# Encoder, mixer A: rotary sines through a second, pair-swapped copy, and the product with v for two heads at a time

## The chip, the core and the metric

The kernel runs on one core of a Trainium2 chip. The metric is the device time of one execution in microseconds (us). A core has five engines with a queue of instructions each, worked off in order: TensorE (PE in the profile; its weight loads are shown as PEld), VectorE (DVE), ScalarE (ACT), GpSimd (POOL) and SyncE (SP), which here only starts transfers. Matmuls write to PSUM, which ScalarE and VectorE can read; all else is in SBUF.

## The reference

A trunk of two layers over 256 positions of width 2048, in float32. Layer 0 mixes tokens with mixer A, layer 1 with mixer B; after each comes a gated MLP with a depthwise convolution. The change lies in mixer A alone: grouped-query attention with 16 query heads, 4 heads for k and v, head width 128, normalised q and k, and a rotation by position of each half of a head.

```python
def rot(xs, pos):                      # a half of a head, 64 wide; quarter = 32
    ang = pos[:, None] * inv_freq[None, :]
    x1, x2 = xs[..., :quarter], xs[..., quarter:]
    return jnp.concatenate([x1 * cos - x2 * sin, x2 * cos + x1 * sin], axis=-1)
...
q = axial_rope(rms_norm(q, q_gain)); k = axial_rope(rms_norm(k, k_gain))
logits = jnp.einsum('bqkgd,bskd->bkgqs', q_blk, k) * scale
p = jax.nn.softmax(logits, axis=-1)
o = jnp.einsum('bkgqs,bskd->bqkgd', p, v)
```

So each element of the rotated q or k is itself times a cosine plus its partner, 32 columns away, times a sine with a sign.

## The kernel before

Each float32 factor is split into a high part in a reduced format and the low rest, and a product is made of three matmuls (high by high, low by high, high by low). Weights stream from HBM in pieces of 128 x 1024 (`raw`, four buffers); ScalarE writes the high part `wh` (L156), VectorE the rest `wl` (L157), four buffers each. `feed` uses a piece in 12 matmuls (L144 to L146) that add into two accumulators in PSUM, `acc`, one for each half of the 256 positions (m = 0, 1).

Mixer A projects k and v first, then q in four groups of four heads. What follows a projection is written as a generator, and between matmuls of the next projection `step()` takes it to its next `yield`, so that the small work runs beside the next group's weights. A scheduler then orders each engine's queue by its own estimates; weight splits have a higher priority.

After k or a group of q, `qk_post` runs:

- ScalarE writes `stg`, the accumulators times the token's scale (L477, two activations of 512 columns), and `sq`, their squares (L591).
- GpSimd multiplies `stg`, with pairs swapped, by the signed sines `st` into `t2`: four operations of 256 columns (L597), one for each m and each half of a pair.
- VectorE multiplies `stg` by the cosines `ct` into `ro` (L600), adds `t2` (L602), sums the squares by head (L603) and prepares the norm (L272), which GpSimd finishes with a power (L273).

For a group of q, `attend` transposes `ro` on TensorE (L494), splits it into `qT` (L196 on ScalarE, L197 on VectorE), and then goes through six steps, k = 0 to 5, in two halves each. In the first half of step k it computes the scores of head k (L210 to L212, 6 matmuls), the maximum on VectorE (L646, L648), the exponential on ScalarE (L652), and the division by the sum on GpSimd (L656). In the second half, head k-1's probabilities are transposed on TensorE (L665) and split into `pT` (two buffers), and head k-2's product with v runs: 6 matmuls of 256 columns (L210 to L212, via `mm3`) into a PSUM tile of its own, split into the head's slots `ah`, `al`. A group's last steps fall into the projection of the next group, whose `qk_post` is queued between them.

The tables of cosines and sines are made at the start from `rp` (the rope table) and `gbs` (the gains), which share buffers with `pT`.

Of the kernel before, what the change touches and what calls it, by code (L numbers as in the profile page):

```python
# [7 lines left out]
F32 = mybir.dt.float32  # L8
F32R = mybir.dt.float32r
AF = mybir.ActivationFunctionType  # L10
ALU = mybir.AluOpType
AX = mybir.AxisListType

P = 128
D = 2048
NT = 256
# [12 lines left out]
def tile_encoder(ctx: ExitStack, tc: tile.TileContext, x, xT, w_a, w_ao, q_gain, k_gain, w_b, w_bo,  # L29
                 rel_bias, gains, w_up, conv, w_down, final_norm, rope, ident_c, onehot, out):  # L30
    nc = tc.nc
# [24 lines left out]
    def nm(s):  # L56
        uid[0] += 1
        return f"{s}_{uid[0]}"

    def ps_tile():  # L60
        return psp.tile([P, 512], F32, tag="ps", name=nm("ps"))
# [3 lines left out]
    def copy(o, i):  # L65
        turn[0] ^= 1
        if turn[0]:
            nc.scalar.activation(o, i, AF.Copy)
        else:
            nc.vector.tensor_copy(o, i)  # L70
# [121 lines left out]
    def split(hi, lo, src):  # L192
        if lo is None:
            copy(hi, src)
            return
        nc.scalar.activation(hi, src, AF.Copy)  # L196
        nc.vector.tensor_tensor(lo, src, hi.bitcast(F32), ALU.subtract)  # L197
# [7 lines left out]
    def mm3(o, lhsT, rhs, ls, rs, start, stop):  # L205
        (lh, ll), (rh, rl) = lhsT, rhs
        if ll is None:
            nc.tensor.matmul(o, lh[ls], rh[rs], start=start, stop=stop)  # L208
            return
        nc.tensor.matmul(o, lh[ls], rh[rs], start=start, stop=False)  # L210
        nc.tensor.matmul(o, lh[ls], rl[rs], start=False, stop=False)  # L211
        nc.tensor.matmul(o, ll[ls], rh[rs], start=False, stop=stop)  # L212

    def pair_tile(pool, shape, tag, bufs=1, whole=False):
        if whole:
            return pool.tile(shape, F32, tag=tag + "h", name=nm(tag), bufs=bufs), None
        return tuple(pool.tile(shape, F32R, tag=tag + c, name=nm(tag + c), bufs=bufs) for c in "hl")
# [9 lines left out]
    def new_slots(kts):  # L227
        return {kt: new_slot(kt) for kt in kts}
# [40 lines left out]
    def rsqrt_mean(dst, ss, n, eps=EPS):  # L269
        w = ss.shape[-1]  # L270
        ms = small.tile([P, w], F32, tag="ms", name=nm("ms"))
        nc.vector.tensor_scalar(ms, ss, 1.0 / n, eps, op0=ALU.mult, op1=ALU.add)  # L272
        nc.gpsimd.tensor_tensor(dst, ms, nhalf[:, :w], ALU.pow)  # L273
# [200 lines left out]
    def evac_scaled(pool, accs, rstd, bufs=2):  # L474
        o = pool.tile([P, 2, 512], F32, tag="stg", name=nm("stg"), bufs=bufs)
        for m in range(2):
            nc.scalar.activation(o[:, m, :], accs[m], AF.Copy, scale=rstd[:, m:m + 1])  # L477
        return o

    def evac_split(pool, accs, rstd, whole=False):  # L480
        hi, lo = pair_tile(pool, [P, 2, 512], "v", 1, whole)
        for m in range(2):
            split_scaled(hi[:, m, :], lo if lo is None else lo[:, m, :], accs[m], rstd[:, m:m + 1])
        return hi, lo
# [25 lines left out]
    def mixer_a():  # L510
        with tc.tile_pool(name="apool", bufs=1) as ap:
# [1 line left out]
            hT, ss_in = {}, new_ss()  # L513
            kgs = list(range(4))

            rp = ap.tile([P, 2, 2, P], F32, tag="pTh", name="rp", bufs=2)
            gbs = ap.tile([P, 4, P], F32, tag="pTl", name="gbs", bufs=2)
            tabs = {}
            rstd = []

# [59 lines left out]
                    load_x(1)  # L580

            def qk_post(accs, which, keep, scale=1.0):
                s = evac_scaled(ap, accs, rstd[0], 1)
                ct, st = tabs[which]
                ssq = small.tile([P, 8], F32, tag="ssq", name=nm("ssq"))
                r = small.tile([P, 8], F32, tag="rqk", name=nm("rqk"), bufs=3)
                ro = ap.tile([P, 2, 512], F32, tag="ro", name=nm("ro"))
                t2 = ap.tile([P, 2, 512], F32, tag="t2", name=nm("t2"))
                sq = ap.tile([P, 2, 512], F32, tag="sq", name=nm("sq"))
                for m in range(2):  # L590
                    nc.scalar.activation(sq[:, m, :], accs[m], AF.Square, scale=rstd[0][:, m:m + 1])  # L591
                rv, sv = (t.rearrange("p m (a c) -> p m a c", a=4) for t in (ro, s))
                for m in range(2):
                    t5, s5 = (t[:, m, :].rearrange("p (a f e c) -> p a f e c", a=4, f=2, e=2) for t in (t2, s))
                    st5 = st[:, m, :].rearrange("p (f e c) -> p f e c", f=2, e=2)
                    for e in range(2):
                        nc.gpsimd.tensor_tensor(t5[:, :, :, e, :], s5[:, :, :, 1 - e, :],  # L597
                                                st5[:, None, :, e, :].to_broadcast([P, 4, 2, 32]), ALU.mult)
                yield
                nc.vector.tensor_tensor(rv, sv, ct[:, :, None, :].to_broadcast([P, 2, 4, P]), ALU.mult)  # L600
                yield
                nc.vector.tensor_tensor(ro, ro, t2, ALU.add)  # L602
                nc.vector.tensor_reduce(ssq, sq.rearrange("p m (a c) -> p (m a) c", a=4), axis=AX.X, op=ALU.add)  # L603
                rsqrt_mean(r, ssq, P * scale * scale, EPS / (scale * scale))
                keep.extend((ro, r))

            slots = new_slots(range(16))
# [15 lines left out]
            v = evac_split(ap, va, rstd[0])  # L623
# [3 lines left out]
            def attend(g, accs):  # L627
                keep = []
                yield from qk_post(accs, "q", keep, SCALE)
                ro, rq = keep  # L630
                rqv = rq.rearrange("p (m a) -> p m a", m=2)
                qT = pair_tile(ap, [P, 4, NT], "qT")
                yield
                for _ in heads_T(qT, ro):
                    pass
                prs, pTs, ots = {}, {}, {}
                for k in range(6):
                    yield
                    if k < 4:
                        i = k  # L640
                        s = ps_tile()
                        for m in range(2):
                            mm3(s[:, m * NT:(m + 1) * NT], qT, kT,
                                (slice(None), i, slice(m * P, (m + 1) * P)), (slice(None), g), True, True)
                        mx = small.tile([P, 2], F32, tag="mx", name=nm("mx"), bufs=3)
                        nc.vector.tensor_reduce(mx, s.rearrange("p (m c) -> p m c", m=2), axis=AX.X,  # L646
                                                op=ALU.max, negate=True)
                        nc.vector.tensor_tensor(mx, mx, rqv[:, :, i], ALU.mult)  # L648
                        pr = ap.tile([P, 2, NT], F32, tag="pr", name=nm("pr"), bufs=2)
                        l = small.tile([P, 2], F32, tag="l", name=nm("l"), bufs=3)  # L650
                        for m in range(2):
                            nc.scalar.activation(pr[:, m, :], s[:, m * NT:(m + 1) * NT], AF.Exp,  # L652
                                                 bias=mx[:, m:m + 1], scale=rq[:, 4 * m + i:4 * m + i + 1],
                                                 accum_out=l[:, m:m + 1])
                        nc.vector.reciprocal(l, l)
                        nc.gpsimd.tensor_tensor(pr, pr, l[:, :, None].to_broadcast([P, 2, NT]), ALU.mult)  # L656
                        prs[i] = pr
                    yield "half"
                    if 1 <= k < 5:
                        i = k - 1  # L660
                        pr = prs.pop(i)
                        t = ps_tile()
                        for m in range(2):
                            for kt in range(2):
                                nc.tensor.transpose(t[:, kt * NT + m * P:kt * NT + (m + 1) * P],  # L665
                                                    pr[:, m, kt * P:(kt + 1) * P], ident)
                        pTs[i] = pair_tile(ap, [P, 2 * NT], "pT", 2)
                        split(pTs[i][0], pTs[i][1], t)
                    if k >= 2:
                        i = k - 2  # L670
                        pT = pTs.pop(i)
                        ot = ps_tile()[:, :NT]
                        for kt in range(2):
                            mm3(ot, v, pT, (slice(None), kt, slice(g * P, (g + 1) * P)),
                                (slice(None), slice(kt * NT, (kt + 1) * NT)), kt == 0, kt == 1)
                        hi, lo = slots[4 * g + i]
                        split(hi, lo, ot)

            for g in range(4):
                start(attend(g, project(w_a, g, hT, kgs)))  # L680
# [258 lines left out]
```

## Time and profile before

| | us |
|---|---|
| median of 3 runs (2294.59 to 2295.15) | 2294.7 |
| the profiled execution | 2294.99 |
| its span, first to last instruction | 2293.2 |
| TensorE busy | 2280.3 |
| VectorE busy | 1631.3 |
| ScalarE busy | 1218.1 |
| GpSimd busy | 170.3 |

How to read it: an engine's busy time is the union of its instructions' times. A matmul's time includes its way through the array and overlaps with its neighbours', so the start of one to the start of the next says what it costs in a run. In a row of groups stand line, engine, operation, output <- inputs, shape and count, then busy us and mean ns, then the idle time before them and what ended it. In a row of the timeline stand start us, duration us, engine, line, operation, and the idle time before it with its releaser. In a row of waits stand who waited for whom, us in total, times and the longest. In a row of stages stand the stretch, its length, then busy us and count for PE, PEld, DVE, ACT and POOL, TensorE's granted clock, the share of the DMA engines and GB/s. A row of one line's instructions gives the shortest, median and longest in ns, then the first and last start. In the critical chain stand start, duration and what.

### The profile page before, as it was taken

The page shows a single profiled execution, that of the slowest core. Times are in us where ns is not written, and L with a number is a line of the kernel's source. Part 1 is how long each engine was busy: PE and PEld are TensorE (multiplying, and loading weights), DVE is VectorE, ACT ScalarE, POOL GpSimd, SP SyncE. Part 2 cuts the span into 40 slices and gives each one's busy share as a digit, 9 for nine tenths or more (in the row PEclk, how much of TensorE's full clock was granted, in tenths as well). Part 3 has the DMA queues.
Part 4 walks back from the last instruction along what each step waited for, and adds up shares of the span by engine and source line. Part 5 has one row for each costly group of instructions (what it writes and reads, how often), then busy time and mean ns, then how long its engine had stood idle before and what let it go on. Part 6 is the DMA issues. An engine that isn't in the chain of part 4 may idle for free.

```text
span 2293.2 us, 31100 instructions
## 1 busy us (share of the span) xinstructions
PE 2280.3 (99%) x11641; PEld 1947.1 (85%) x11641; DVE 1631.3 (71%) x2284; ACT 1218.1 (53%) x1746; POOL 170.3 (7%) x170
## 2 busy tenths in 40 slices
PE   9999999999999999999999999999999999999998
PEld 7888888888888888888888888888888888888886
DVE  6877877776457776878866875676777744777754
ACT  7565565554345555545454554445555533555543
POOL 2331101110000000010000000000000000000010
PEclk9999999999999999999999999999999999999999
DMA  8535656765555555566555554566555565555554
GB/s 299 166 131 164 202 190 206 214 213 194 194 194 184 192 190 189 188 216 210 185 175 181 178 189 163 178 198 206 189 189 189 188 194 193 191 190 187 192 191 149
DMA packets 261447, 437.57 MB, mean 191 GB/s; under 512 B 17216, under 2 KB 198208, under 8 KB 261168
## 3 DMA queue, kind: packets, MB, share of 16 engines
q1 hardware_dynamic: 254912, 425.64, 56.6%
q0 software_dynamic: 5952, 9.38, 1.6%
q8 instruction: 91, 1.49, 0.3%
q10 hardware_dynamic: 432, 0.56, 0.1%
q14 instruction: 60, 0.49, 0.1%
HBM read 429.20 MB, written 6.29 MB: 190 GB/s over the span
## 4 chain that ended last, share of the span: by engine, by line
PE 97%; DVE 1%; DMA 0%; issue 0%; POOL 0%; ACT 0%; SPq 0%; POOLq 0%; DVEq 0%; ACTq 0%
PE acc L123 28%; PE acc L145 17%; PE acc L146 17%; PE acc L144 17%; PE acc L121 15%; PE ps L208 1%; PE ps L211 1%; PE ps L212 0%; PE ps L210 0%; DMA raw<-in_w_a_dram 0%; DVE wl L157 0%; PE ps L665 0%; PE ps L815 0%; DVE tT L237 0%; POOL t L597 0%
## 5 line engine op out<-in xcount | busy, mean ns | idle before, releaser
L157 DVE TENSOR_TENSOR wl<-raw,wh 128x1024 fp32r<-128x1024 f32 (+1 forms) x456 | 553.5, 1216 | 320.1 <-ACT wh L156 316.2
L156 ACT ACTIVATE wh<-raw 128x1024 fp32r<-128x1024 f32 (+1 forms) x456 | 475.0, 1045 | 514.5 <-PE acc L146 449.6
L123 PE MATMUL acc<-xh,wh 128*128 128x512 f32 x2816 | 674.2, 391 | 0.0
L123 PEld LDWEIGHTS acc<-xh,wh 128*128 128x128 f32 x2816 | 517.0, 188 | 99.9 <-DVE v L356 0.4
L112 DVE TENSOR_TENSOR wl<-raw,wh 128x1024 fp32r<-128x1024 f32 x352 | 457.9, 1301 | 196.6 <-ACT wh L111 196.6
L111 ACT ACTIVATE wh<-raw 128x1024 fp32r<-128x1024 f32 x352 | 372.0, 1058 | 208.4 <-issue 70.9
L144 PE MATMUL acc<-wh,ah 128*128 128x512 f32 x1024 | 399.3, 390 | 0.0
L145 PE MATMUL acc<-wl,ah 128*128 128x512 f32 x1024 | 398.8, 389 | 0.0
L146 PE MATMUL acc<-wh,al 128*128 128x512 f32 x1024 | 398.7, 389 | 0.0
L121 PEld LDWEIGHTS acc<-xh,wl 128*128 128x128 f32 x2816 | 361.8, 191 | 14.2
L121 PE MATMUL acc<-xh,wl 128*128 128x256 f32 x2816 | 366.7, 283 | 0.0
L144 PE MATMUL acc<-wh,xh 128*128 128x512 f32 x768 | 302.7, 395 | 1.9 <-ACT wh L156 1.9
L145 PE MATMUL acc<-wl,xh 128*128 128x512 f32 x768 | 300.0, 391 | 0.2 <-DVE wl L157 0.2
L146 PE MATMUL acc<-wh,xh 128*128 128x512 f32 x768 | 299.8, 390 | 0.0
L146 PEld LDWEIGHTS acc<-wh,al 128*128 128x128 f32 x1024 | 192.2, 188 | 40.0
L144 PEld LDWEIGHTS acc<-wh,ah 128*128 128x128 f32 x1024 | 192.3, 188 | 39.4
L145 PEld LDWEIGHTS acc<-wl,ah 128*128 128x128 f32 x1024 | 192.3, 188 | 39.3
L146 PEld LDWEIGHTS acc<-wh,xh 128*128 128x128 f32 x768 | 144.2, 188 | 30.4
L144 PEld LDWEIGHTS acc<-wh,xh 128*128 128x128 f32 x768 | 144.4, 188 | 30.0 <-ACT wh L156 2.3
L145 PEld LDWEIGHTS acc<-wl,xh 128*128 128x128 f32 x768 | 144.4, 188 | 27.8 <-DVE wl L157 0.5
L375 POOL TENSOR_TENSOR cv<-cg,cv 128x512 f32<-128x512 f32 x44 | 63.5, 1444 | 1101.9 <-DVE cv L367 1101.9
L355 ACT ACTIVATE v<-acc 128x256 f32<-128x256 f32 x176 | 65.8, 374 | 108.5 <-PE acc L123 108.5
(156 smaller groups left out, 1385.8 us busy)
## 6 DMA issues: line engine op xcount, KB each, us to landing
raw<-in_w_up_dram SPq DMA_DIRECT2D x352, 512.0 KB, 3.7
raw<-in_w_down_dram SPq DMA_DIRECT2D x176, 512.0 KB, 3.6
raw<-in_w_b_dram SPq DMA_DIRECT2D x144, 512.0 KB, 3.8
raw<-in_w_bo_dram SPq DMA_DIRECT2D x48, 512.0 KB, 3.6
raw<-in_w_a_dram SPq DMA_DIRECT2D x40, 512.0 KB, 4.3
raw<-in_w_ao_dram SPq DMA_DIRECT2D x32, 512.0 KB, 3.7
raw<-in_w_a_dram SPq DMA_DIRECT2D x16, 256.0 KB, 6.1
h<-in_x_dram SPq DMA_DIRECT2D x4, 512.0 KB, 7.9
```

What stands on the lines that cost most here:

```text
L111: nc.scalar.activation(wh, rk, AF.Copy)
L112: nc.vector.tensor_tensor(wl, rk, wh.bitcast(F32), ALU.subtract)
L121: nc.tensor.matmul(acc[j][:, :NT], wl[:, kt, c], lhs[4 * kg + kt][0], start=st, stop=sp)
L123: nc.tensor.matmul(acc[j], wh[:, kt, c], lhs[4 * kg + kt][2], start=st, stop=sp)
L144: nc.tensor.matmul(accs[m], xh[:, c], wh[:, j, :], start=st, stop=False)
L145: nc.tensor.matmul(accs[m], xh[:, c], wl[:, j, :], start=False, stop=False)
L146: nc.tensor.matmul(accs[m], xl[:, c], wh[:, j, :], start=False, stop=sp)
L156: nc.scalar.activation(wh[:, c], r[:, c], AF.Copy)
L157: nc.vector.tensor_tensor(wl[:, c], r[:, c], wh[:, c].bitcast(F32), ALU.subtract)
L208: nc.tensor.matmul(o, lh[ls], rh[rs], start=start, stop=stop)
L355: nc.scalar.activation(v[:, j], acc[j][:, NT:], AF.Copy)
L375: nc.gpsimd.tensor_tensor(cv, cg, cv, ALU.mult)
```

## The change

`qk_post` first has ScalarE write the accumulators a second time, scaled, straight into `t2`, with the two 32-column halves of each pair swapped by the order in which they are read (two activations of 512 columns). `stg` and `sq` follow as before. GpSimd then multiplies `t2` in place by the sines, for both m and all four heads in one operation of 1024 columns.

In `attend` the transposed probabilities of two heads share one tile, so that the second factor of the product with v is 512 columns: at steps 3 and 5, ahead of that step's transposes, 6 matmuls of 512 columns make the products of two heads, in place of 6 of 256 columns for one head at each of the steps 2 to 5. `pT` then has one buffer for two heads in place of two for one head each. `rp` moves to the buffer of `sq`, and `gbs` has one buffer.

```diff
-            rp = ap.tile([P, 2, 2, P], F32, tag="pTh", name="rp", bufs=2)
-            gbs = ap.tile([P, 4, P], F32, tag="pTl", name="gbs", bufs=2)
+            rp = ap.tile([P, 2, 2, P], F32, tag="sq", name="rp")
+            gbs = ap.tile([P, 4, P], F32, tag="pTl", name="gbs")
...
             def qk_post(accs, which, keep, scale=1.0):
+                t2 = ap.tile([P, 2, 512], F32, tag="t2", name=nm("t2"))
+                for m in range(2):
+                    o, a = (t.rearrange("p (a e c) -> p a e c", a=8, e=2) for t in (t2[:, m, :], accs[m]))
+                    nc.scalar.activation(o, a[:, :, ::-1, :], AF.Copy, scale=rstd[0][:, m:m + 1])
                 s = evac_scaled(ap, accs, rstd[0], 1)
...
-                for m in range(2):
-                    t5, s5 = (t[:, m, :].rearrange("p (a f e c) -> p a f e c", a=4, f=2, e=2) for t in (t2, s))
-                    st5 = st[:, m, :].rearrange("p (f e c) -> p f e c", f=2, e=2)
-                    for e in range(2):
-                        nc.gpsimd.tensor_tensor(t5[:, :, :, e, :], s5[:, :, :, 1 - e, :],
-                                                st5[:, None, :, e, :].to_broadcast([P, 4, 2, 32]), ALU.mult)
+                t4 = t2.rearrange("p m (a c) -> p m a c", a=4)
+                nc.gpsimd.tensor_tensor(t4, t4, st[:, :, None, :].to_broadcast([P, 2, 4, P]), ALU.mult)
...
                     yield "half"
+                    if k in (3, 5):
+                        i = k - 3
+                        pT = [p.rearrange("p k a c -> p k (a c)") for p in pTs.pop(i // 2)]
+                        ot = ps_tile()
+                        for kt in range(2):
+                            mm3(ot, v, pT, (slice(None), kt, slice(g * P, (g + 1) * P)),
+                                (slice(None), kt), kt == 0, kt == 1)
+                        for j in range(2):
+                            split(*slots[4 * g + i + j], ot[:, j * NT:(j + 1) * NT])
                     if 1 <= k < 5:
...
-                        pTs[i] = pair_tile(ap, [P, 2 * NT], "pT", 2)
-                        split(pTs[i][0], pTs[i][1], t)
-                    if k >= 2:
-                        i = k - 2
-                        pT = pTs.pop(i)
-                        ot = ps_tile()[:, :NT]
-                        for kt in range(2):
-                            mm3(ot, v, pT, (slice(None), kt, slice(g * P, (g + 1) * P)),
-                                (slice(None), slice(kt * NT, (kt + 1) * NT)), kt == 0, kt == 1)
-                        hi, lo = slots[4 * g + i]
-                        split(hi, lo, ot)
+                        if i % 2 == 0:
+                            pTs[i // 2] = [ap.tile([P, 2, 2, NT], F32R, tag="pT" + c, name=nm("pT" + c))
+                                           for c in "hl"]
+                        split(*(p[:, :, i % 2, :] for p in pTs[i // 2]), t.rearrange("p (k c) -> p k c", k=2))
```

In the program built from the changed kernel, the queues around the start of a later group stand as follows. ScalarE: the exponentials of head 3, `ah`, `pT` of head 2, `t2`, `ah`, `t2`, `stg` twice, `sq` twice, `pT` of head 3, then two weight splits. VectorE: `al`, `pT` of head 2, `al`, L600, L603, `pT` of head 3, two weight splits, `al`, L602. TensorE: scores of head 3, 6 weight matmuls, the first pair's product, transposes of head 2, 12 weight matmuls, transposes of head 3, 12 weight matmuls, the second pair's first matmul (L210), two weight matmuls, L211 and the rest of the pair, 16 weight matmuls, L494 of the next group. Around the first group VectorE has L600, a weight split, L602, a split, L603, a split, L272, a split, `qT`. (Line numbers are those of the kernel before.)

More of the change, by code (lines that the diff above doesn't have):

```diff
@@ L587, in qk_post @@
                 ro = ap.tile([P, 2, 512], F32, tag="ro", name=nm("ro"))
-                t2 = ap.tile([P, 2, 512], F32, tag="t2", name=nm("t2"))
                 sq = ap.tile([P, 2, 512], F32, tag="sq", name=nm("sq"))
@@ L635, in attend @@
                     pass
-                prs, pTs, ots = {}, {}, {}
+                prs, pTs = {}, {}
                 for k in range(6):
```

## The prediction

> **What bounds the kernel now.** First the page: busy time by engine, then the chain that ended last; then the same shares cut by stage, the waits of the stage that the change touches, and the matmuls around the one wait found there.
>
> ```profile
> span 2293.2 us, 31100 instructions
> PE 2280.3 (99%) x11641; PEld 1947.1 (85%) x11641; DVE 1631.3 (71%) x2284; ACT 1218.1 (53%) x1746; POOL 170.3 (7%) x170
> PE 97%; DVE 1%; DMA 0%; issue 0%; POOL 0%; ACT 0%; SPq 0%; POOLq 0%; DVEq 0%; ACTq 0%
> ```
> ```profile
> 44.00:76.00 32.00, 32.00 (x143) 26.48 (x142) 27.80 (x37) 17.76 (x21) 7.43 (x6) 1.00 0.61 198
> 76.00:108.00 32.00, 31.43 (x170) 26.47 (x169) 25.24 (x35) 21.29 (x41) 14.72 (x13) 1.00 0.48 157
> 108.00:139.00 31.00, 31.00 (x172) 26.38 (x171) 23.68 (x36) 19.86 (x39) 10.78 (x10) 1.00 0.42 137
> ...
> PE ps L494 <- DVE ro L602: 0.6, 1, 0.6
> ```
> ```profile
> 81.65 0.39 PE L145 MATMUL acc<-wl,xh 128*128 128x512 f32 x1
> 81.88 0.39 PE L146 MATMUL acc<-wh,xh 128*128 128x512 f32 x1
> 82.84 1.09 PE L494 MATMUL ps<-ident,ro 128*128 128x128 f32 x8 [0.57 <-DVE ro L602]
> ```
>
> TensorE is the bound everywhere: 99% of the span, at the full clock (1.00) in mixer A. Its only visible loss in the stage that changes is one wait: L494, the first transposes of the rotated q, could have started 0.23 after 81.88, at 82.11, and starts at 82.84, so 0.73 us are lost. Whatever the change takes off the other engines is therefore worth at most 0.73 us; whatever it puts into TensorE's queue as a wait is lost in full, since there is no idle time behind it to win it back.
>
> **The change part by part.**
>
> *Product with v for two heads.* 96 matmuls of 256 columns (6 for each of 16 heads) become 48 of 512. The mean time of one (283 and 391 ns) overlaps with its neighbours'; what counts is the spacing, in a run of 16 of 256 and then of 512 columns:
>
> ```profile
> L121 PE MATMUL acc<-xh,wl 128*128 128x256 f32 x2816 | 366.7, 283 | 0.0
> L123 PE MATMUL acc<-xh,wh 128*128 128x512 f32 x2816 | 674.2, 391 | 0.0
> ...
> 315.89 1.92 PE acc L121 x16
> 317.81 3.65 PE acc L123 x16
> ```
> 1.92/16 = 0.120 and 3.65/16 = 0.228, so two short ones give way to one long one at a gain of 0.012 us: 48 x 0.012 = 0.6 us off TensorE. The splits of the product keep their number and size. But head 0's product moves one step later and runs with head 1's, and head 2's runs with head 3's: the last product of a group now needs the transposed probabilities of head 3 (pT) for all its columns.
>
> *GpSimd, one multiplication for four.*
>
> ```profile
> L530 POOL TENSOR_TENSOR ct_k<-rp,gbs x2: 457/458/458, 25.3 to 26.3; 128x128 f32<-128x128 f32 x2
> L597 POOL TENSOR_TENSOR t<-stg,st_q x16: 730/739/1730, 75.1 to 168.6; 128x256 f32<-128x256 f32 x16
> L656 POOL TENSOR_TENSOR pr<-pr,l x16: 1039/1040/1042, 90.9 to 195.1; 128x512 f32<-128x512 f32 x16
> L375 POOL TENSOR_TENSOR cv<-cg,cv x44: 1282/1294/2143, 295.9 to 2182.7; 128x512 f32<-128x512 f32 x44
> L375 POOL TENSOR_TENSOR cv<-cg,cv 128x512 f32<-128x512 f32 x44 | 63.5, 1444 | 1101.9 <-DVE cv L367 1101.9
> ```
> The shortest times lie on a line: 457, 730, 1282 ns for 128, 256, 512 columns, 2.15 ns a column and 0.18 us on top. 1024 columns give 0.18 + 2.20 = 2.4 us undisturbed. Below it stands two times L656, 2.1 us; above, two times L375's mean, 2.9. I take 2.6, between the line and the mean, because one long operation meets VectorE more easily than a short one. The Trainium skill (GPSIMD Engine Reference, "Elementwise — side-by-side cycle accounting") gives 4497 ns for 2048 columns, so an estimate of 2.25 us here; by that the sum below would be 1.4 us lower, 0.35 in four places.
>
> *What that operation does to VectorE* is seen where the second group of heads starts now. ACT, DVE, POOL, then TensorE without its weight matmuls:
>
> ```profile
> 102.95 0.39 ACT L196 ACTIVATE ah<-ps 128x256 fp32r<-128x256 f32 x1
> 103.22 1.28 ACT L477 ACTIVATE stg<-acc,rstd 128x512 f32<-128x512 f32 x2
> 104.36 1.29 ACT L591 ACTIVATE sq<-acc,rstd 128x512 f32<-128x512 f32 x2
> 105.49 0.65 ACT L196 ACTIVATE pTh<-ps 128x512 fp32r<-128x512 f32 x1
> ```
> ```profile
> 104.53 1.78 DVE L600 TENSOR_TENSOR ro<-stg,ct_q 128x1024 f32<-128x1024 f32 x1 [0.73 <-ACT stg L477]
> 106.24 1.21 DVE L603 TENSOR_REDUCE ssq<-sq 128x8 f32<-128x1024 f32 x1
> 107.37 0.67 DVE L197 TENSOR_TENSOR pTl<-ps,pTh 128x512 fp32r<-128x512 f32 x1
> ```
> ```profile
> 104.50 3.80 POOL L597 TENSOR_TENSOR t<-stg,st_q 128x256 f32<-128x256 f32 x4
> L600 DVE TENSOR_TENSOR ro<-stg,ct_k x1: 1224/1224/1224, 47.7 to 47.7; 128x1024 f32<-128x1024 f32 x1
> ```
> ```profile
> 98.58 0.28 PE L210 MATMUL ps<-kTh,qTh 128*128 128x256 f32 x1
> 100.68 0.60 PE L665 MATMUL ps<-ident,pr 128*128 128x128 f32 x4
> 101.04 0.36 PE L210 MATMUL ps<-pTh,vh 128*128 128x256 f32 x1
> 108.56 0.28 PE L210 MATMUL ps<-pTh,vh 128*128 128x256 f32 x1
> 108.68 0.28 PE L211 MATMUL ps<-pTl,vh 128*128 128x256 f32 x1
> ```
> L600 takes 1.22 us alone and 1.78 here. The first of GpSimd's four operations began at 104.50 and, at 0.74, ended near 105.24; L600 ended at 106.31, 1.07 after it. So VectorE stood until GpSimd's operation was through and then ran, and GpSimd's other three waited in turn. The Trainium skill (SBUF — State Buffer, "Who interferes with whom") has this as a rule: a VectorE instruction with two SBUF inputs and a GpSimd one that reads SBUF exclude each other for the whole instruction. The trace agrees (1.78 against 1.22).
>
> Today's four short operations let VectorE in after 0.74 us. The one long operation starts before L600 can (its input t2 is written ahead of stg) and holds VectorE for its whole length. Behind L600 on VectorE's queue stand the reduction and then pTl of head 3, for which the pair's product waits.
>
> *The boundary between two groups, worked out.* Now: ScalarE's block starts at 103.22 and pTl ends at 108.04, 4.82 later; L211 wants it at 108.68: 0.64 us to spare. Changed: ScalarE writes t2, ah, t2, then stg, stg. At 0.57 an activation (half of 1.28 overlaps), 0.30 for ah and 0.70 for the second t2 to end, t2 is complete 1.57 after the block's start. GpSimd 2.6: 4.17. L600 1.07: 5.24. The reduction 1.13 (106.24 to 107.37): 6.37. pTl 0.67: 7.04. TensorE from the first score matmul of head 3 (98.58) to L211 (108.68): 10.10 now. In the changed queue the first pair's 6 long matmuls (1.37) replace 12 short ones (1.44), and ahead of L211 stand one long one and two weight matmuls that the scheduler put between (0.68) instead of one short (0.12): 10.6. The block starts 4.64 after 98.58 now. I put it 0.36 later: without head 0's product (0.72) the scores of head 3 come nearer to GpSimd's multiplication of head 2's probabilities, which then holds the weight split ahead of the maximum. So pTl is there at 4.64 + 0.36 + 7.04 = 12.04, 0.06 more for the hand-over, and TensorE stands 12.10 - 10.60 = 1.5 us at L211. There are three such boundaries (the fourth group has none behind it): 3 x 1.5 = 4.5 us. Without the 0.36 each is 1.1.
>
> *The first group.* VectorE and ScalarE today:
>
> ```profile
> 76.17 1.40 DVE L600 TENSOR_TENSOR ro<-stg,ct_q 128x1024 f32<-128x1024 f32 x1 [0.28 <-ACT stg L477]
> 77.50 1.21 DVE L603 TENSOR_REDUCE ssq<-sq 128x8 f32<-128x1024 f32 x1
> 78.63 3.02 DVE L157 TENSOR_TENSOR wl<-raw,wh 128x1024 fp32r<-128x1024 f32 x2
> 81.57 1.21 DVE L602 TENSOR_TENSOR ro<-ro,t 128x1024 f32<-128x1024 f32 x1
> 85.06 1.27 DVE L197 TENSOR_TENSOR qTl<-ps,qTh 128x512 fp32r<-128x512 f32 x2
> ...
> 74.31 0.67 ACT L477 ACTIVATE stg<-acc,rstd 128x512 f32<-128x512 f32 x1
> ```
> The changed order is t2, stg, t2, stg on ScalarE: t2 complete at 74.31 + 2 x 0.57 + 0.70 = 76.15, GpSimd to 78.75, L600 to 79.82. VectorE's queue then has a weight split, L602, a split, the reduction, two splits, qTl, at about 1.14 each: L602 ends at 82.1, just when L494 wants it, so the 0.73 goes; the first qTl ends at 87.3. L212, the first score matmul that needs it, is due at 82.11 + 0.95 (8 transposes, 82.84 to 83.69, and 0.1 of turning back) + 12 weight matmuls 2.72 + 0.24 = 86.0: a new wait of 1.3. Net 1.3 - 0.73 = +0.6.
>
> *Free parts.* The ten added activations: 0.57 each on ScalarE, 21.29 of 32 us busy; weights lie ahead of their use (VectorE's second split above ends at 81.65, TensorE's weight matmuls that use it come after the first scores, past 86). If that cover went, a boundary would pay 1.14. A reversed order of 32-column pieces is not in the trace: I price it as stg's, 0.70; twice that is the upper end, nothing below stg. K's rotation: VectorE waits for 2.6 where it waited in parts, and L602 has no matmul next to it. The tables rp and gbs lie in other buffers, written and read long before. No DMA is added or moved.
>
> *Sum.* -0.6 + 0.6 + 4.5 = +4.5 us, on the profiled execution's 2294.99 us (span 2293.2 and 1.8 around it), which lies 0.3 above the median 2294.7: 2299.5.
>
> **The rivals.**
>
> 1. VectorE isn't held, or only briefly. Then L600 follows stg at once: pTl is ready about 1.3 us earlier at each boundary, the three waits shrink to 0.2, qTl is in time and the 0.73 goes: -0.6 - 0.7 + 0.6 = -0.7, 2294.3, no change. For it: L603 and pTl don't read two SBUF tiles. Against: 1.78 against 1.22.
> 2. The price of the busy time is real: if a matmul of 256 columns cost its mean of 283 ns and one of 512 its 391, 96 x 0.283 - 48 x 0.391 = 8.4 us would go instead of 0.6, and with the waits the time is 2294.99 - 8.4 + 0.6 + 4.5 = 2291.7, not slower; only with no wait either would it be 2286.6. It turns the sign if a short one's spacing in the product is over 0.17 (96 x 0.05 gained). Against: L210 and L211 start 0.12 apart (108.56, 108.68).
> 3. ScalarE's reversed copies cost twice 0.70: t2 comes 1.4 later at three boundaries, and GpSimd with it, and 1.4 in the first group: +5.6, 2305.1. For it only that the trace has no such read.
> 4. The holding operation is shorter (2.1 us): three boundaries 1.0 each, the first group +0.1: -0.6 + 0.1 + 3.0 = +2.5, 2297.5, within the bound.
>
> **How the numbers follow.** 0.2% of this kernel is 4.6 us, about what a measurement of it can tell from no change, and the forecast lies on that edge. Chances: the forecast's waits 0.62, of which 0.44 at or above the edge and 0.18 below, since 2.6 us and the 0.36 can each be less; rival 4 0.10; rival 1 0.10; rival 3 and other costs that lengthen the chain ahead of GpSimd 0.14; rival 2 0.04, half of it with no waits. Hence slower 0.58, same 0.40, faster 0.02. The predicted time is the forecast's, 2299.5; its own range is 2297.5 (rival 4) to 2301.5 (2.9 us for GpSimd, 0.3 more in four places, and 0.2 for each boundary). For 8 in 10: down to 2296.5, which leaves out rivals 1 and 2, and up to 2303.5, part of the way to rival 3.
>
> **What would show it.** Right: GpSimd's multiplication as one operation of 2.4 to 2.7 us, five times; the product at L600's place (ro from stg) 2.3 us or more; matmuls of 512 columns from pT with a wait at L211 on VectorE's pTl of 1 to 1.5 us, three times; no wait at L494 but one at L212 on qTl. Wrong: the pair's products start with no wait (rival 1 or 4), copies into t2 well above 0.70 us (rival 3), or TensorE gains more than 0.6 us in the product (rival 2).

## The result and the profile after

The changed kernel takes 2300.2 us (median of 12 runs), the kernel before 2294.9 beside it (12 runs): 5.3 us slower, ratio 1.0025 with a 95% interval of 1.0018 to 1.0032. The forecast was 2299.5, slower by 4.5 to 4.8. The interval leaves out 1.0000, and it takes in 1.0020, the edge on which the prediction saw its forecast. The profiled execution took 2300.01 us. Its page, the span, the busy times and the chain of waits that ended last:

```profile
span 2298.2 us, 31008 instructions
PE 2281.6 (99%) x11593; PEld 1944.9 (85%) x11593; DVE 1637.2 (71%) x2284; ACT 1222.7 (53%) x1756; POOL 160.1 (7%) x155
PE 97%; DVE 1%; ACT 1%; issue 1%; DMA 0%; POOL 0%; SPq 0%; POOLq 0%; DVEq 0%; ACTq 0%
```

The shares of the page hardly move; 5 us of 2298 do not show in them. The waits of TensorE from 76 to 205 us do show the change (before, this list held the 0.6 us at L494 alone; code lines from `qk_post` on have moved by one or more):

```profile
PE ps L211 <- DVE pTl L197: 3.5, 3, 1.2
PE ps L212 <- DVE qTl L197: 1.1, 1, 1.1
PE ps L673 <- POOL pr L655: 0.2, 1, 0.2
PE ps L494 <- DVE ro L601: 0.2, 1, 0.2
```

The start of the second group, from the timeline of the changed kernel: ScalarE's copies into `t2`, GpSimd, VectorE, then TensorE.

```profile
103.73 0.70 ACT L586 ACTIVATE t<-acc,rstd 128x512 f32<-128x512 f32 x1
104.56 0.72 ACT L586 ACTIVATE t<-acc,rstd 128x512 f32<-128x512 f32 x1
...
105.36 2.40 POOL L597 TENSOR_TENSOR t<-t,st_q 128x1024 f32<-128x1024 f32 x1 [0.79 <-ACT t L586]
...
106.47 2.37 DVE L599 TENSOR_TENSOR ro<-stg,ct_q 128x1024 f32<-128x1024 f32 x1 [1.31 <-ACT stg L477]
109.89 0.67 DVE L197 TENSOR_TENSOR pTl<-ps,pTh 128x512 fp32r<-128x512 f32 x1
...
98.71 0.28 PE L210 MATMUL ps<-kTh,qTh 128*128 128x256 f32 x1
109.02 0.39 PE L145 MATMUL acc<-wl,xh 128*128 128x512 f32 x1
110.62 0.50 PE L211 MATMUL ps<-pTl,vh 128*128 128x512 f32 x1 [1.21 <-DVE pTl L197]
110.96 0.39 PE L212 MATMUL ps<-pTh,vl 128*128 128x512 f32 x1
```

GpSimd's one operation ends at 107.76. The product with the cosines, now L599, starts in the trace at 106.47 and ends at 108.84, 1.08 after GpSimd: it takes 2.37 us, where it took 1.22 alone. Then come the reduction and `pTl`, and L211 starts 1.60 after the weight matmul before it instead of 0.23: 1.37 us lost. The view of waits counts from the modelled end of a matmul, which is 0.16 after the next one could have started, so its 3.5 for three such waits is 3.5 + 3 x 0.16 = 4.0 us of TensorE.

The first group, in the same views:

```profile
76.97 3.02 DVE L599 TENSOR_TENSOR ro<-stg,ct_q 128x1024 f32<-128x1024 f32 x1 [0.86 <-ACT stg L477]
...
81.75 0.39 PE L146 MATMUL acc<-wh,xh 128*128 128x512 f32 x1
82.32 1.09 PE L494 MATMUL ps<-ident,ro 128*128 128x128 f32 x8 [0.18 <-DVE ro L601]
86.12 0.28 PE L211 MATMUL ps<-kTl,qTh 128*128 128x256 f32 x1
87.53 0.39 PE L212 MATMUL ps<-kTh,qTl 128*128 128x256 f32 x1 [1.13 <-DVE qTl L197]
87.75 0.28 PE L210 MATMUL ps<-kTh,qTh 128*128 128x256 f32 x1
```

L494 still waits 82.32 - 81.75 - 0.23 = 0.34 us, and L212 waits 87.53 - 86.12 - 0.12 = 1.29.

### The profile page after: what moved, and what is told of

Read it like the earlier page. It is cut to its first block, busy times and chain, and to the rows that moved or that the text cites. A ratio compares the mean times of both kernels' runs of the same rounds, so it can differ in the third digit from the quotient of the medians.

```text
span 2298.2 us, 31008 instructions
## 1 busy us (share of the span) xinstructions
PE 2281.6 (99%) x11593; PEld 1944.9 (85%) x11593; DVE 1637.2 (71%) x2284; ACT 1222.7 (53%) x1756; POOL 160.1 (7%) x155
## 4 chain that ended last, share of the span: by engine, by line
PE 97%; DVE 1%; ACT 1%; issue 1%; DMA 0%; POOL 0%; SPq 0%; POOLq 0%; DVEq 0%; ACTq 0%
PE acc L123 28%; PE acc L146 17%; PE acc L144 17%; PE acc L145 17%; PE acc L121 15%; PE ps L208 1%; PE ps L211 0%; PE ps L212 0%; PE ps L210 0%; DVE wl L157 0%; PE ps L816 0%; DMA raw<-in_w_a_dram 0%; DVE ro L599 0%; ACT t L586 0%; PE ps L673 0%
## 5 line engine op out<-in xcount | busy, mean ns | idle before, releaser
L121 PEld LDWEIGHTS acc<-xh,wl 128*128 128x128 f32 x2816 | 361.8, 191 | 14.2
L121 PE MATMUL acc<-xh,wl 128*128 128x256 f32 x2816 | 366.7, 283 | 0.0
```

What stands on the lines that cost most here:

```text
L121: nc.tensor.matmul(acc[j][:, :NT], wl[:, kt, c], lhs[4 * kg + kt][0], start=st, stop=sp)
```

## The experiments

The theory under test: one GpSimd operation of 2.4 us keeps VectorE's product with the cosines from running, and pT of head 3 behind it ("hold theory"). Its rivals: the pair product makes the wait, ScalarE's added copies do, or the two engines only slow each other down. Times stand against the kernel before on the same chip (2294.9, in the last two groups of runs 2295.0 and 2294.8).

**One part alone.** The kernel before with the new end of `attend` only:

```diff
-                        pTs[i] = pair_tile(ap, [P, 2 * NT], "pT", 2)
+                        if i % 2 == 0:
+                            pTs[i // 2] = [ap.tile([P, 2, 2, NT], F32R, tag="pT" + c, ...) for c in "hl"]
...
+                    if k in (3, 5):     # product with v, 512 columns
```

> The product with v for two heads at a time alone, on the rotation of the kernel before (four GpSimd operations of 256 columns, no second copy). Hold theory (the one long GpSimd operation keeps VectorE's product with the cosines, L599, from running): nothing here holds VectorE for long, so there is no wait at L211 over 0.2 us, the wait at L494 (0.73) stays, and 48 long matmuls for 96 short ones give 0.4 to 0.6 us: the ratio to before is 0.9997 to 1.0000. Rival (the pair product makes the wait, since it needs head 3's transposed probabilities for all its columns): waits of over 1 us at L211 at three boundaries, 3 to 4.5 us slower than before, 1.0013 to 1.0020.

and the changed kernel with `attend` as it was before:

> The second copy and the one GpSimd operation alone; the product with v one head at a time as before. Hold theory: L599 again 2.3 us or more at the boundaries, waits of 1.1 to 1.5 us on pTl three times, 1.3 on qTl in the first group: 4 to 6 us slower than before, 1.0017 to 1.0026. Rival (the pair product makes the wait): at most the first group's 0.6 us, 1.0000 to 1.0004.

The pair product alone: 2295.5 us, 1.0003 (0.9994 to 1.0012). The rotation alone: 2300.3, 1.0023 (1.0013 to 1.0032). TensorE's list in mixer A holds, for the pair product, the 0.6 at L494 and nothing else, as before; for the rotation among others:

```profile
PE ps L211 <- DVE pTl L197: 3.0, 3, 1.0
```

The loss is the rotation's; the pair product alone makes no wait that this list shows. It doesn't show its 0.6 us either: its ratio lies above the 0.9997 to 1.0000 that were expected, and only the interval reaches there. Two parts of this can be seen. In its profiled execution TensorE lost 1 us in the MLP, at L121, because a piece of weights landed late. And inside mixer A, from the first activation that empties the accumulators of v to the first matmul of the MLP, it gains no more than 210.38 - 210.12 = 0.26. Before, then with the pair product and its wait at L211 in the second group:

```profile
51.71 0.69 ACT L200 ACTIVATE vh<-acc,rstd 128x512 fp32r<-128x512 f32 x1 [0.98 <-PE acc L146]
262.09 1.98 PE L123 MATMUL acc<-xh,wh 128*128 128x512 f32 x8
```
```profile
51.14 0.69 ACT L200 ACTIVATE vh<-acc,rstd 128x512 fp32r<-128x512 f32 x1 [0.97 <-PE acc L146]
...
107.13 0.39 PE L210 MATMUL ps<-pTh,vh 128*128 128x512 f32 x1
107.39 0.19 PEld L211 LDWEIGHTS ps<-pTl,vh 128*128 128x128 f32 x1 [0.30 <-DVE pTl L197]
107.73 0.39 PE L212 MATMUL ps<-pTh,vl 128*128 128x512 f32 x1
...
261.26 1.98 PE L123 MATMUL acc<-xh,wh 128*128 128x512 f32 x8
```

L211 just has to wait for `pTl` here, too briefly for the list: its weight load and its matmul start at 107.39, 0.26 after L210, and L212 starts 0.34 after that, instead of 0.23 each. That is 0.14 us, and 0.4 over the three boundaries. Without these starts the gain would be 0.66, close to the 0.6 forecast.

**Who is held, and by what.** VectorE takes its product out of PSUM, all else as in the changed kernel:

```diff
-                nc.vector.tensor_tensor(rv, sv, ct[:, :, None, :].to_broadcast([P, 2, 4, P]), ALU.mult)
+                for m in range(2):
+                    nc.vector.scalar_tensor_tensor(rv[:, m], accs[m].rearrange("p (a c) -> p a c", a=4),
+                        rstd[0][:, m:m + 1], ct[:, m, None, :].to_broadcast([P, 4, P]), ALU.mult, ALU.mult)
```

> The changed kernel, but VectorE makes the product with the cosines out of the accumulators in PSUM, with the token's scale, in two operations of 512 columns; only one of its large inputs is then in SBUF. ScalarE's work stays as it is: stg is still written, and nobody reads it. Hold theory, with the hold tied to two SBUF inputs: the two products take about 0.7 us each (1.4 together) beside GpSimd's 2.4, the waits at L211 are under 0.2 and the one at L212 under 0.4; the time is that of before, 0.9996 to 1.0003. Rival (ScalarE's two added copies make the chain late, by 1.14 us, whatever VectorE reads): waits at L211 of about 1.2 stay, 4 us or more slower than before, 1.0017 or more.

2296.7 us, 1.0007 (0.9998 to 1.0016).

```profile
L600 DVE SCALAR_TENSOR_TENSOR ro<-acc,rstd,ct_q x8: 737/746/753, 78.0 to 168.5; 128x512 f32<-128x512 f32 x8
PE ps L494 <- DVE ro L604: 1.0, 1, 1.0
```

The waits at L211 and L212 are gone from TensorE's list with ScalarE's work unchanged. No product takes over 0.753 us, though GpSimd's operation runs beside the first of each two (k's two, with GpSimd idle, took 0.731 and 0.737). The rival with ScalarE's copies falls. Input, operation and length changed together, so the run shows that this form isn't held, and not which of the three frees it.

The ratio lies above the 0.9996 to 1.0003 that were expected; only its interval reaches in. Of the 1.7 us by which the profiled span grew, mixer A holds 0.7: above all, the first group's wait at L494 is longer (1.0 in this view, 0.6 before), since the two products start late there. Another 0.9 lie behind the last matmul, where nothing was changed, and stay open.

Next, GpSimd's operation cut in two, one for each half of the positions, and then only the second of these halves:

```diff
-                nc.gpsimd.tensor_tensor(t4, t4, st[:, :, None, :].to_broadcast([P, 2, 4, P]), ALU.mult)
+                for m in range(2):      # second experiment: m = 1 alone
+                    nc.gpsimd.tensor_tensor(t4[:, m], t4[:, m], st[:, m, None, :].to_broadcast([P, 4, P]), ALU.mult)
```

> The changed kernel with GpSimd's multiplication in two operations of 512 columns, one for each half of the positions. By the line of the rows each takes about 1.28 us, and the first starts 0.6 us earlier, when the first of the two copies is there. Hold theory: L599 arrives in the second and is held for the rest of it, about 0.4 us instead of 1.3; the waits at L211 fall from 1.45 to 0.4 to 0.7, so the kernel is 1 to 2.5 us slower than before, 1.0004 to 1.0011. Rival (ScalarE's copies make the chain late): unchanged, 4 to 5.5 us slower, 1.0017 to 1.0024. Rival (the hold is only contention for the same memory, in proportion to the overlap): L599 is longer by as much as GpSimd's two operations overlap it, and the waits change by less than 0.4.

> The changed kernel with GpSimd's multiplication for the second half of the positions only: 512 columns, about 1.29 us, from the same start. The first half's multiplication with the sines is left out, so the rotation of these positions is not computed. Hold theory, one for one: the operation ends 1.1 us earlier, so L599 is held for 0.2 us instead of 1.3; the waits at L211 fall from 1.35 to 0.2 to 0.3, the one at L212 from 1.29 to 0.1 to 0.3, and the one at L494 (0.34) goes; 2295 to 2296. Rival (the price is set by the two added copies on ScalarE, which are the same): the waits stay.

Two halves: 2297.4 us, 1.0013 (1.0004 to 1.0022), 2.45 us slower, at the upper end of the 1 to 2.5 that were expected. One half, without the sines for the first half of the positions: 2295.4 in a single run. VectorE's product and GpSimd's operations, in the first and in the second of these kernels:

```profile
L600 DVE TENSOR_TENSOR ro<-stg,ct_q x4: 1372/1676/1680, 76.9 to 168.5; 128x1024 f32<-128x1024 f32 x4
L598 POOL TENSOR_TENSOR t<-t,st_q x8: 1289/1292/2277, 75.2 to 167.8; 128x512 f32<-128x512 f32 x8
PE ps L211 <- DVE pTl L197: 1.5, 3, 0.5
```
```profile
L599 DVE TENSOR_TENSOR ro<-stg,ct_q x4: 1258/1259/1908, 76.3 to 166.6; 128x1024 f32<-128x1024 f32 x4
L597 POOL TENSOR_TENSOR t<-t,st_q x4: 1282/1284/1293, 75.9 to 165.5; 128x512 f32<-128x512 f32 x4
```

With 1.11 us less of GpSimd's operation (2.40 to 1.28) the product at a boundary is 1.11 shorter (2.37 to 1.26): one for one, as a hold gives. At a shared half rate, the 1.29 us that the two overlapped in the changed kernel (106.47 to 107.76) would have cost the product 0.65; they cost 1.15. No wait of TensorE on VectorE is left in mixer A's list; by the spacing of starts 0.23 us remain at each boundary, as expected, of 1.37. The first group's product, 1.91, still overlaps its hold.

**The order of ScalarE's copies.** The added copies behind `sq`, so that VectorE runs first:

> The changed kernel with ScalarE's two added copies moved behind stg and sq, nothing else. GpSimd then has nothing to multiply until VectorE's L599 runs. Hold theory: L599 is back at 1.2 us at the three later boundaries and its GpSimd operation comes after it, so no wait at L211 over 0.2; in the first group t2 comes late and is itself put back by VectorE's weight split, so the wait moves to L494, 1.5 to 2.5 us there, none at L212; in all 0.5 to 1.5 us slower than before, 1.0002 to 1.0007. Rival (the number of activations ahead of pT of head 3 decides, which is the same): 4 us or more, 1.0017.

2304.5 us, 1.0038 (1.0025 to 1.0051): the hold theory, as I had put it, fails here. The rival's bound is met, by far more than it gave a reason for. The waits, and the second group's start on GpSimd and VectorE:

```profile
PE ps L211 <- DVE pTl L197: 5.2, 3, 1.7
PE ps L494 <- DVE ro L601: 2.2, 1, 2.2
...
107.91 2.38 POOL L597 TENSOR_TENSOR t<-t,st_q 128x1024 f32<-128x1024 f32 x1 [3.10 <-ACT t L594]
...
105.56 1.22 DVE L599 TENSOR_TENSOR ro<-stg,ct_q 128x1024 f32<-128x1024 f32 x1 [0.16 <-ACT stg L477]
107.97 2.36 DVE L272 TENSOR_SCALAR ms<-ssq 128x8 f32<-128x8 f32 x1
110.24 0.68 DVE L197 TENSOR_TENSOR pTl<-ps,pTh 128x512 fp32r<-128x512 f32 x1
```

L599 is free (1.22), as expected. But L272, eight columns from one input, stands for 2.36 us until GpSimd is through, and `pTl` behind it. I had tied the hold to two inputs in SBUF; that is too narrow. The Trainium skill (SBUF — State Buffer, "Who interferes with whom") names the operation of L272, `tensor_scalar`, among those that can contend with GpSimd for the pair of ports that it shares with VectorE; the trace agrees (2.36 beside GpSimd, 0.16 where L272 runs alone). To see whether L272 is the cause and not only the place, it goes to GpSimd:

```diff
-        nc.vector.tensor_scalar(ms, ss, 1.0 / n, eps, op0=ALU.mult, op1=ALU.add)
+        (eng or nc.vector).tensor_scalar(ms, ss, 1.0 / n, eps, op0=ALU.mult, op1=ALU.add)   # eng = nc.gpsimd in qk_post
```

> The kernel with the added copies last, and beside it the small step L272 (mean of squares plus epsilon, 8 columns) of the rotation on GpSimd instead of VectorE. There the trace showed L272, with one input of 8 columns, standing for 2.35 us beside GpSimd's multiplication, with pT of head 3 behind it. If this hold is what made the waits of 1.9 us at L211, they are gone here (under 0.2). In the first group GpSimd now does the power ahead of the multiplication, so that L494 waits 1 us longer, 3.3 to 3.7. In all 2 to 3 us slower than before, 1.0008 to 1.0013, against 1.0038 with L272 on VectorE. Rival (the later copies themselves make the chain late, and L272's length is only where it shows): the waits at L211 stay at 1.9, 1.004 or more.

2301.0 us, 1.0029 (1.0017 to 1.0042). TensorE's whole list in mixer A, three starts after the wait (three matmuls lie between the last two), and two stretches, in which the granted clock stands behind GpSimd's busy time:

```profile
PE ps L494 <- DVE ro L601: 4.0, 1, 4.0
...
85.79 1.97 PE L494 MATMUL ps<-ident,ro 128*128 128x128 f32 x8 [4.03 <-DVE ro L601]
87.41 0.78 PE L144 MATMUL acc<-wh,xh 128*128 128x512 f32 x1
89.25 0.40 PE L145 MATMUL acc<-wl,xh 128*128 128x512 f32 x1
...
86.50:87.50 1.00, 1.00 (x7) 1.00 (x5) 1.00 (x2) 0.56 (x1) 0.00 (x0) 0.50 0.05 16
89.50:90.50 1.00, 1.00 (x6) 0.84 (x5) 0.00 (x0) 0.00 (x0) 0.00 (x0) 1.00 0.56 180
```

The three waits at L211 are gone from the list: L272 made them. The time came out above the 1.0008 to 1.0013 expected. Two reasons lie in the first group: L272 and the power take GpSimd longer than I had put, so L494 waits 4.0 and not 3.3 to 3.7; and after that wait TensorE's clock is at 0.50 for 3.4 us. Eight transposes take 1.62 us there (0.85 in the changed kernel) and the next four matmuls 1.84 instead of 1.01: 1.6 us on top of the wait. The profiled execution, 2300.0, is 1.0 below the median; where the others lost that us wasn't seen.

**What the first group lost.** GpSimd's operation for k alone in two halves:

> The changed kernel with GpSimd's multiplication for k alone in two operations of 512 columns; those for q stay whole. The prediction took k's rotation to cost nothing. If it does cost, through k's turn on VectorE, which ends later, and ScalarE's kTh behind it (72.62 instead of 72.40), then kTh starts 0.2 us earlier here, t2 of the first group too, and the wait at L494 falls from 0.34 to 0.1 to 0.2; the waits at L211 (1.33 to 1.38) stay. If k's rotation costs nothing, all waits stay as in the changed kernel. One GpSimd instruction is added as well, so the late division of the fourth group may move.

2300.0 us in a single run. ScalarE's split of k's turn, in the changed kernel and here, and here TensorE's list:

```profile
72.62 1.07 ACT L196 ACTIVATE kTh<-tT 128x1024 fp32r<-128x1024 f32 x1 [2.98 <-DVE tT L237]
```
```profile
72.32 1.06 ACT L196 ACTIVATE kTh<-tT 128x1024 fp32r<-128x1024 f32 x1 [2.46 <-DVE tT L237]
PE ps L211 <- DVE pTl L197: 3.5, 3, 1.2
```

The wait at L494 is gone, those at L211 are as they were, and the one at L212 is 1.0 in this view: k's rotation was not free.

**A late start on GpSimd.** In the fourth group the division of head 0, L655, started 0.5 us after the reciprocal that releases it, in the changed kernel, and TensorE stood 0.35 us for it. One GpSimd instruction more, far ahead:

> The changed kernel with one GpSimd instruction more, long before: the first multiplication that makes the table of k's cosines is cut into two of half the columns. In three kernels with the same number of GpSimd instructions, the same one (the division L655 of head 0 in the fourth group) starts 0.51 us after its release instead of 0.17, and TensorE loses 0.35 us at the transposes behind it; in kernels with more GpSimd instructions ahead it does not. If the place in GpSimd's queue makes it late, the late start falls on the instruction one earlier, the power L273 of the fourth group, by the same 0.34 us, and the wait at the transposes (0.35) is gone, for 0.3 to 0.4 us less. Rival (what the other engines do at that time makes it late): the division starts late again, and nothing changes.

2300.4 us in a single run. Release and start in the changed kernel, then with one more:

```profile
187.09 0.17 DVE L654 RECIPROCAL l<-l 128x2 f32<-128x2 f32 x1 [1.33 <-ACT pr L651]
187.77 1.04 POOL L655 TENSOR_TENSOR pr<-pr,l 128x512 f32<-128x512 f32 x1 [6.51 <-PE ps L212]
```
```profile
187.50 0.17 DVE L658 RECIPROCAL l<-l 128x2 f32<-128x2 f32 x1 [1.33 <-ACT pr L655]
187.83 1.04 POOL L659 TENSOR_TENSOR pr<-pr,l 128x512 f32<-128x512 f32 x1 [6.17 <-PE ps L212]
```

0.51 (187.77 - 187.26) against 0.16: the late start and TensorE's wait are gone, with the other engines' work there unchanged. It did not pass to the power one earlier, though, which starts 0.08 after its release in both. The division is this late in the five kernels here with as many GpSimd instructions ahead of it as the changed one, and in none with more. So the late start goes with their number; why stays open.

**What the runs point to,** in one kernel: the pair product, the copy with pairs swapped, the product out of PSUM without `stg`, GpSimd in two halves.

> What the runs so far point to, put together: product with v for two heads, the pair-swapped copy, the product with the cosines out of PSUM with stg left out altogether, and GpSimd's multiplication in two operations of 512 columns. Hold theory: VectorE's two products take 0.75 us each whatever GpSimd does, GpSimd starts 0.6 us earlier and has 1.14 less of ScalarE ahead of it; no wait at L211, L212 or L494 over 0.2 us, so TensorE saves the 0.4 to 0.6 us of the pair product and the 0.73 at L494: 2293.5 to 2294.2, 0.9995 to 0.9998. If another cost was hidden (PSUM read by VectorE and ScalarE at once, accumulators given back later): a wait shows at the first weight matmuls of a group or at L494, and the time is that of before or above.

2293.4 us, 1.6 below the kernel before, ratio 0.9993 (0.9984 to 1.0002): the interval just takes in no change, so a gain isn't shown by the times alone. In its trace nothing of the change is left to wait for; TensorE's list is empty from 15 to 300 us, where it had 0.6 at L494 before. The stretch of mixer A:

```profile
51.01 0.69 ACT L200 ACTIVATE vh<-acc,rstd 128x512 fp32r<-128x512 f32 x1 [0.98 <-PE acc L146]
259.97 1.98 PE L123 MATMUL acc<-xh,wh 128*128 128x512 f32 x8
```

It takes 208.96 us, 1.42 less than before. The wait at L494 was 0.73 of that, which leaves 0.69 for the pair product, whose L211 waits for nothing here.

## Why the prediction was right, and where its terms were off

It was right, by its mechanism: VectorE's product is held until the one GpSimd operation is through, pT of head 3 comes late, and TensorE pays at L211 three times and at L212 once. That the number came out so near is in part luck, as the sum below shows.

- *The boundary.* Of the worked-out chain, ScalarE's first copy was put at 5.00 us after the first score of head 3 and came at 5.02 (103.73 - 98.71); `t2` complete 1.57 later, measured 1.55; from GpSimd's end to that of VectorE's product 1.07, measured 1.08. GpSimd's operation was the term that was mis-sized: 2.6 us by choice, 2.40 measured; the line through the shorter operations gave 2.38, and VectorE did not lengthen it. The estimate from the Trainium skill's cycle counts (GPSIMD Engine Reference, "Elementwise — side-by-side cycle accounting"), 2.25, was 0.15 short. So the waits are 4.0 us in all, not 4.5.
- *The first group.* Put at +0.6, measured 1.29 + 0.34 - 0.73 = +0.9. The step that failed is "the 0.73 goes": half of it stayed, since k's rotation, counted as free, ended 0.2 to 0.3 us later.
- *Left out.* After each of these waits the next matmul starts 0.34 after the first one instead of 0.23 (110.62 to 110.96; at L212 0.22 instead of 0.12): 0.4 us over four waits. The late division costs 0.35.
- *The pair product.* Put at -0.6. Alone, mixer A shows 0.26, since the product then just waits at L211 three times (0.4 in all); where it waits for nothing, in the last kernel, 0.69 is left for it. So the term fits, but the slack at L211 was smaller than the list of waits suggests.
- *Sum.* 4.0 + 0.9 + 0.4 + 0.35 - 0.6 = 5.05; the medians differ by 5.3 and the two spans by 5.0. The forecast of 4.5 was that near because a term 0.5 too large stood against 1.05 us of terms too small or left out.
- *The rivals.* 1 (no hold) falls with 2.37 us for L599, 2 (the price of busy time) with 0.7 us gained at most, where it asked for 8.4, 3 (reversed copies cost twice) with 0.70 us a copy. 4 (a shorter hold) lay nearly halfway: 2.40. A start of the pair's product without a wait is named as a sign of rival 4 too; by that rival's own sum it would have left 1.0 us at each boundary.

## What to carry to other kernels

Fewer, longer GpSimd operations are no gain in themselves: a VectorE product with two SBUF inputs, and even a step of eight columns, stood here until GpSimd's multiplication of 2.4 us was through, and everything queued behind them too. So look for what VectorE has queued next, small steps included. Taking one input from PSUM gave most of the time back here (2296.7 for 2300.2), cutting the long operation in two about half of it (2297.4). On an engine that is the bound all the time, price matmuls by the spacing of their starts, and a wait by that spacing too: a list of waits can leave out the short ones.

## What the runs showed of the hardware that I had not expected

- A VectorE step of eight columns (L272, a tensor with a scalar) stood 2.36 us beside GpSimd's operation, as long as one of 1024 columns did.
- Not every GpSimd operation holds. Beside the power L273, which runs 2.54 us on eight columns, a weight split with two SBUF inputs started and ended in its usual 1.2 us (changed kernel):

```profile
178.72 2.54 POOL L273 TENSOR_TENSOR rqk<-ms,nhalf 128x8 f32<-128x8 f32 x1 [7.21 <-DVE ms L272]
...
180.64 1.23 DVE L157 TENSOR_TENSOR wl<-raw,wh 128x1024 fp32r<-128x1024 f32 x1 [0.87 <-ACT wh L156]
```

- After a wait of 4.0 us TensorE was granted half its clock for 3.4 us (matmuls of 512 columns 0.41 to 0.43 apart instead of 0.23), which cost 1.6 us on top; after the 2.2 us at L494 in the kernel with the copies last, the next eight transposes took 0.85 as usual. The Trainium skill (TensorE: Matmul & The Clock Gate, "Part 1: The HAM clock gate") has half the clock after an idle window of about 3.4 us and the full one after as long a busy stretch; the trace agrees with both, on either side of that length.
- After a wait of TensorE, however short, the next matmul of 512 columns starts 0.33 to 0.34 after the first one instead of 0.23 (L211 to L212 at the boundaries, changed kernel and pair product alone).
- The late start on GpSimd, 0.51 us instead of 0.16 after its release, which goes with the number of instructions ahead in its queue.
